# Two gate panels of the first mixer streamed through the head, with wider conditioning dots

## The chip, the core and the metric

The kernel runs on one core of a Trainium2 chip. The metric is the device time of one execution in microseconds (us). Three runs of the kernel before took 2177.68 to 2180.78 us, median 2178.91. Five engines work side by side, each through its own list in order: PE (matrix products), DVE (vector), ACT (ScalarE, functions and copies), POOL, and SP, which here only issues transfers.

## What is computed

A trunk of two layers over x of 256 rows and 2048 columns, with a condition c. Only the first half of layer 0 matters here:

```
shift, scale, gate, ... = split(silu(c) @ ada_w + ada_b)
h  = x * (1 + scale) + shift
xa, ga, ub, vb = split(h @ w_in)            # 1024 columns each
ya = rg_lru(conv(xa)) * gelu(ga)
yb = gelu(ub) * spatial(layer_norm(gelu(vb)))
x  = layer_norm(alpha * x + (1 + gate) * (concat(ya, yb) @ w_out))
```

Then an FFN, and a second layer with another mixer. All weights are fp32, and the largest ones are read once, so every weight passes from memory through the chip in the order in which it is used.

## The kernel before

A product is done in panels of 512 columns (`nb`) and chunks of 512 rows of the weight (`ch`); one weight block of a panel and a chunk is 1 MB. Such a block is loaded into one of the four buffers of `p_raw` (`load_raw`), and split into a high and a low part (`split`, L84 on ACT and L85 on DVE, two halves of 1024 columns each). PE then does three products a piece (`products`, L161 to L163), 24 for a block with its two halves of rows (`tb`). A few blocks aren't split but multiplied in fp32 (`products32`, L152).

The conditioning vectors (`mods`) are made by **dots**: `ada_dot` loads 1 MB of `ada_w` into a buffer of the same four, multiplies it by `silc` on DVE and sums each row; it does so in two halves of 1024 columns (L99), and `ada_final` adds the two sums and the bias (L104 to L109).

Mixer 0 (`mixer_ab`) begins with the **head**: 16 blocks of rows (`kb`), four to a chunk. For each block two dots give scale and shift, x is modulated on DVE (L545), and PE adds six fp32 products to six PSUM banks that stay open (panels 0, 1 and 6; L547: a head group). From the second chunk on, `stream` takes the panels 7, 4 and 5 for the chunk before, one behind each of the first three blocks: products into one of two banks `hs`, then a copy (first chunk, ACT, L524) or an add (DVE, L526) into an accumulator in SBUF, and a gelu after the last chunk. Behind the head the three streams run for the fourth chunk.

Then `linear` runs over the two **gate panels** 2 and 3, chunks in the order 2, 3, 0, 1, adding up in PSUM; its first two blocks are fp32 products (`RAW_GA`). Between the blocks `todo` places the convolution inputs, the two halves of the recurrence (`rg_lru`, on ACT and DVE), the norm (`v_norm`) and the spatial products. `evac` multiplies the gate into y. Then comes the **output projection** (`out_proj`): 16 blocks, the first two in fp32, the last four in `close`.

After each block `pump` asks for `RATE_E` = 1.0 more dots of the list `early` (24 dots: the gate of this half, and the first quarter of the next scale and shift); what is left is done two steps before the projection's end. The framework's scheduler sets the order on each engine from the order of the code and its own estimates; the engines then follow it strictly.

Of the kernel before, what the change touches and what calls it, by code (L numbers as in the profile page):

```python
# [13 lines left out]
P = 128  # L14
# [12 lines left out]
RATE_E = 1.0  # L27
QUIET = 2
RAW_GA = (0, 1)
# [13 lines left out]
def trunk_kernel(ctx, tc, I, out):  # L43
# [50 lines left out]
    def ada_dot(acc, l, idx, kb):  # L94
        w = p_raw.tile([P, D], F32, name="w")
        nc.sync.dma_start(w, I["ada_w"][l, idx, kb])
        for hf in range(2):
            cs = slice(hf * 1024, hf * 1024 + 1024)
            V.scalar_tensor_tensor(w[:, cs], w[:, cs], 1.0, silc[:, cs], op0=ALU.mult, op1=ALU.mult,  # L99
                                   accum_out=acc[:, hf:hf + 1])  # L100

    def ada_final(acc, l, s, nm, idx, k0, n):
        m = mods[l, s, nm][:, k0:k0 + n]
        V.tensor_tensor(m, acc[:, :, 0], acc[:, :, 1], op=ALU.add)  # L104
        bias = vc("ab", (6 * l + idx) * KB + k0, n)
        if nm == "sh":
            V.tensor_tensor(m, m, bias, op=ALU.add)
        else:
            V.scalar_tensor_tensor(m, m, 1.0, bias, op0=ALU.add, op1=ALU.add)  # L109
        ln = 2 * l + s - 1  # L110
        if nm == "sh" and ln >= 0:
            sc = mods[l, s, "sc"][:, k0:k0 + n]
            t4 = p_t.tile([P, n], F32, name="t4")
            V.tensor_tensor(t4, vc("nb", ln * 16 + k0, n), sc, op=ALU.mult)
            V.tensor_tensor(m, m, t4, op=ALU.add)
            V.tensor_tensor(sc, sc, vc("ng", ln * 16 + k0, n), op=ALU.mult)

    def ada_tiles(l, s, part, q, n=CH):
        for nm, idx in (("sc", 3 * s + 1), ("sh", 3 * s)) if part == "s" else (("gt", 3 * s + 2),):
            acc = p_t.tile([P, n, 2], F32, name="ga")  # L120
            for j in range(n):
                ada_dot(acc[:, j], l, idx, n * q + j)
                if j == n - 1:
                    ada_final(acc, l, s, nm, idx, n * q, n)
                yield
# [52 lines left out]
    def acc_bank():  # L178
        return psum["acc"].tile([P, NB], F32, name="acc")
# [316 lines left out]
    def mixer_ab(pump):  # L496
        with ExitStack() as st:
# [13 lines left out]
            dst = {7: vg[:, :, NB:], 4: ug[:, :, 0:NB], 5: ug[:, :, NB:]}  # L511

            with tc.tile_pool(name="pshead", bufs=1, space=PSUM) as p8, tc.tile_pool(name="hraw", bufs=3) as p_hr:
                head = [(nb, tb) for nb in (0, 1, 6) for tb in range(2)]
                banks = {k: p8.tile([P, NB], F32, name=f"hd{k[0]}{k[1]}") for k in head}

                def stream(nb, ch):
                    hl = load_w(src(nb, ch))
                    for tb in range(2):
                        bk = p8.tile([P, NB], F32, name=f"hs{tb}")  # L520
                        products(bk, xs[ch], hl, tb, range(2), True, True)
                        d = dst[nb][:, tb]
                        if ch == 0:
                            A.activation(d, bk, AF.Copy)  # L524
                        else:
                            V.tensor_tensor(d, d, bk, op=ALU.add)  # L526
                        if ch == 3:
                            A.activation(d, d, AF.Gelu_apprx_tanh)

                spread(silc, 4, lambda i: p8.tile([P, NB], F32, name=f"hs{i % 2}"), AF.Silu)  # L530
                for kb in range(KB):
# [31 lines left out]
                for nb in (7, 4, 5):  # L563
                    stream(nb, 3)
                    pump()
# [38 lines left out]
            def evac(nb, tb, bk):  # L604
                j = nb - 2
                ts = slice(tb * P, tb * P + P)
                e = p_t.tile([P, NB], F32, name="t512")
                A.activation(e, bk, AF.Gelu_apprx_tanh)
                pt = transposed(e, 4)
                V.tensor_tensor(y[j][:, :, ts], y[j][:, :, ts], pt, op=ALU.mult)  # L610
# [22 lines left out]
            def v_norm():  # L633
                for tb in range(2):
# [6 lines left out]
            todo = {1: lambda: (conv_in(0), conv_in(1)), 2: lambda: rg_lru(0), 4: v_norm,  # L641
                    5: lambda: (spatial(0), spatial(1)), 6: lambda: rg_lru(1)}
            count = [0]

            def pump2():
                count[0] += 1
                pump()
                if count[0] in todo:
                    todo[count[0]]()
# [140 lines left out]

    class Pump:
# [123 lines left out]
```

## Time and profile before

| | |
|---|---|
| three runs | 2177.68, 2178.91, 2180.78 us |
| profiled execution: span | 2175.9 us (its own time is not listed beside it; the runs' median lies 3.0 us above this span) |
| PE busy | 2111.6 us, 97% |
| DVE busy | 1618.6 us, 74% |
| ACT busy | 966.5 us, 44% |
| moved by DMA | 601.20 MB, mean 276 GB/s |

How the rows further below are read. On the page, a slice is a fortieth of the span, and a digit is a busy share in tenths. A row of the stages has the stretch and its length, the busy time of PE, PEld (weight loads), DVE, ACT and POOL with the number of instructions, the granted clock of PE as a share of full speed, the share of the DMA engines and GB/s. A row of a timeline or of the chain has start and length in us, then engine, line, operation and what is written from what, and in brackets the idle time before it with its releaser. A row of the groups has the count, busy us and mean ns, then the idle time before. A row of the waits has who waited for whom: us in total, how often, the longest.

### The profile page before, as it was taken

The page shows a single profiled execution, that of the slowest core. Times are in us where ns is not written, and L with a number is a line of the kernel's source. Part 1 is how long each engine was busy: PE and PEld are TensorE (multiplying, and loading weights), DVE is VectorE, ACT ScalarE, POOL GpSimd, SP SyncE. Part 2 cuts the span into 40 slices and gives each one's busy share as a digit, 9 for nine tenths or more (in the row PEclk, how much of TensorE's full clock was granted, in tenths as well). Part 3 has the DMA queues.
Part 4 walks back from the last instruction along what each step waited for, and adds up shares of the span by engine and source line. Part 5 has one row for each costly group of instructions (what it writes and reads, how often), then busy time and mean ns, then how long its engine had stood idle before and what let it go on. Part 6 is the DMA issues. An engine that isn't in the chain of part 4 may idle for free.

```text
span 2175.9 us, 24074 instructions
## 1 busy us (share of the span) xinstructions
PE 2111.6 (97%) x9124; PEld 1666.4 (77%) x9124; DVE 1618.6 (74%) x2202; ACT 966.5 (44%) x1124; POOL 31.5 (1%) x55
## 2 busy tenths in 40 slices
PE   7989999999999999999999999999999999999996
PEld 3556767887888888888868777868888888888885
DVE  7778988899977788889779977666555555555656
ACT  1215733544544445444444556354444444444442
POOL 0000000000000000000000011000000000000000
PEclk9999999999999999999999999999999999999998
DMA  9987787988888888888858877646676666555552
GB/s 399 388 322 267 303 329 297 341 325 336 301 314 312 322 330 322 335 319 312 319 217 311 324 267 292 261 173 221 230 271 229 222 226 233 208 203 193 194 194 91
DMA packets 84747, 601.20 MB, mean 276 GB/s; under 512 B 9444, under 2 KB 9876, under 8 KB 13846
## 3 DMA queue, kind: packets, MB, share of 16 engines
q1 hardware_dynamic: 84630, 599.67, 73.7%
q8 instruction: 71, 1.16, 0.2%
q14 instruction: 46, 0.37, 0.1%
HBM read 597.51 MB, written 2.12 MB: 276 GB/s over the span
## 4 chain that ended last, share of the span: by engine, by line
PE 85%; DVE 9%; ACT 2%; DMA 2%; issue 1%; POOL 1%; SPq 0%; DVEq 0%; ACTq 0%; POOLq 0%
PE acc L162 25%; PE acc L163 25%; PE acc L161 24%; DVE w L99 3%; PE hd L547 3%; PE acc L152 3%; DVE l L85 2%; PE aux L228 2%; DMA w<-in_ada_w 1%; PE hs L162 1%; PE hs L163 1%; PE hs L161 1%; DMA w<-in_w_cd 0%; ACT h L84 0%; POOL z L736 0%
## 5 line engine op out<-in xcount | busy, mean ns | idle before, releaser
L85 DVE TENSOR_TENSOR l<-w,h 128x1024 fp32r<-128x1024 f32 x676 | 822.9, 1223 | 421.4 <-ACT h L84 420.1
L84 ACT ACTIVATE h<-w 128x1024 fp32r<-128x1024 f32 x676 | 711.6, 1059 | 862.0 <-PE acc L163 689.4
L162 PE MATMUL acc<-l,xh 128*128 128x512 f32 x2608 | 1019.2, 391 | 6.2 <-DVE l L85 5.8
L161 PE MATMUL acc<-h,xh 128*128 128x512 f32 x2608 | 1018.2, 392 | 5.9 <-ACT xh L318 4.5
L163 PE MATMUL acc<-h,xl 128*128 128x512 f32 x2608 | 1018.3, 391 | 0.0
L162 PEld LDWEIGHTS acc<-l,xh 128*128 128x128 f32 x2608 | 489.8, 188 | 112.4 <-DVE l L85 11.8
L161 PEld LDWEIGHTS acc<-h,xh 128*128 128x128 f32 x2608 | 489.5, 188 | 108.2 <-ACT xh L318 5.5
L163 PEld LDWEIGHTS acc<-h,xl 128*128 128x128 f32 x2608 | 489.8, 188 | 100.4 <-DVE xl L319 0.3
L99 DVE SCALAR_TENSOR_TENSOR w<-w,silc 128x1024 f32<-128x1024 f32 x384 | 459.0, 1219 | 18.0 <-DMA w<-in_ada_w 15.6
L547 PE MATMUL hd<-w,y 128*128 128x512 f32 x192 | 93.8, 642 | 20.7 <-DVE y L545 20.7
L547 PEld LDWEIGHTS hd<-w,y 128*128 128x128 f32 x192 | 38.4, 205 | 72.7 <-issue 43.2
L85 DVE TENSOR_TENSOR xl<-hid,xh 128x1024 fp32r<-128x1024 f32 x44 | 53.9, 1224 | 34.2 <-ACT xh L84 33.6
L84 ACT ACTIVATE xh<-hid 128x1024 fp32r<-128x1024 f32 x44 | 46.8, 1063 | 63.0 <-PE acc L162 63.0
L152 PE MATMUL acc<-w,hx 128*128 128x512 f32 x96 | 43.1, 599 | 2.8 <-ACT hx L313 2.7
L161 PE MATMUL hs<-h,xh 128*128 128x512 f32 x96 | 40.9, 428 | 0.0
L162 PE MATMUL hs<-l,xh 128*128 128x512 f32 x96 | 39.0, 406 | 0.0
L163 PE MATMUL hs<-h,xl 128*128 128x512 f32 x96 | 38.0, 396 | 0.0
L84 ACT ACTIVATE xh<-y 128x1024 fp32r<-128x1024 f32 x12 | 12.7, 1058 | 56.6 <-DVE y L545 48.6
L152 PEld LDWEIGHTS acc<-w,hx 128*128 128x128 f32 x96 | 17.6, 190 | 23.4 <-issue 17.5
L99 DVE DVE_READ_ACCUMULATOR w<-w,silc 128x1 f32 x384 | 31.3, 82 | 0.0
L152 PE MATMUL acc<-w,y 128*128 128x512 f32 x64 | 28.5, 592 | 0.0
L427 DVE TENSOR_TENSOR hid<-hid,acc 128x512 f32<-128x512 f32 x40 | 27.2, 683 | 1.5 <-PE acc L163 1.4
(207 smaller groups left out, 851.4 us busy)
## 6 DMA issues: line engine op xcount, KB each, us to landing
w<-in_ada_w SPq DMA_DIRECT2D x192, 1024.0 KB, 5.1
w<-in_wg SPq DMA_DIRECT2D x88, 1024.0 KB, 5.2
w<-in_wu SPq DMA_DIRECT2D x88, 1024.0 KB, 5.1
w<-in_wd SPq DMA_DIRECT2D x88, 1024.0 KB, 4.9
w<-in_w_cd SPq DMA_DIRECT2D x32, 1024.0 KB, 6.2
w<-in_w_ab SPq DMA_DIRECT2D x20, 1024.0 KB, 5.2
w<-in_w_ab_out SPq DMA_DIRECT2D x16, 1024.0 KB, 7.0
w<-in_w_cd_out SPq DMA_DIRECT2D x16, 1024.0 KB, 6.7
```

The costliest lines, as they stand in the source:

```text
L84: A.activation(h, src, AF.Copy)
L85: mark["v"] = V.tensor_tensor(l, src, h, op=ALU.subtract)
L99: V.scalar_tensor_tensor(w[:, cs], w[:, cs], 1.0, silc[:, cs], op0=ALU.mult, op1=ALU.mult, accum_out=acc[:, hf:hf + 1])
L152: T.matmul(bk, x[:, k, ts], w[:, k], start=first and k == 0, stop=last and k == 3)
L161: T.matmul(bk, xh[:, k, ts], h[:, j], start=first and k == 0, stop=False)
L162: T.matmul(bk, xh[:, k, ts], l[:, j], start=False, stop=False)
L163: T.matmul(bk, xl[:, k, ts], h[:, j], start=False, stop=last and k == 3)
L228: T.transpose(pt[:, i], src[:, i * P:(i + 1) * P], ident)
L427: V.tensor_tensor(part(nb, tb), part(nb, tb), bk, op=ALU.add)
L547: T.matmul(banks[nb, tb], xt[:, k, tb * P:tb * P + P], w[:, i // 2], start=kb == 0, stop=kb == KB - 1)
```

## The change

- The gate panels 2 and 3 are streamed in the head too: each gets an SBUF accumulator (`ga`, in the buffer of the later row `gb`). Behind the four blocks of a chunk now stand panel 7, panel 4, panels 5 and 2, and panel 3. `RAW_GA` and the loop over the gate panels go; their blocks are all split.
- Behind the head the fourth chunk of the five panels runs with the banks of the later pool (`acc_bank`), with the recurrence, norm and spatial products between; `gate_y` multiplies both gates into y at the end.
- x is modulated on ACT (L541 of the new kernel) instead of DVE.
- A dot is one instruction of 2048 columns (L96), and `ada_final` has one operation less.
- `RATE_E` is 1.6, and the load of x is issued after three pumps of the output projection.

```
-RATE_E = 1.0
+RATE_E = 1.6
-        for hf in range(2):
-            cs = slice(hf * 1024, hf * 1024 + 1024)
-            V.scalar_tensor_tensor(w[:, cs], w[:, cs], 1.0, silc[:, cs], op0=ALU.mult, op1=ALU.mult,
-                                   accum_out=acc[:, hf:hf + 1])
+        V.scalar_tensor_tensor(w, w, 1.0, silc, op0=ALU.mult, op1=ALU.mult, accum_out=acc)
...
-        V.tensor_tensor(m, acc[:, :, 0], acc[:, :, 1], op=ALU.add)
...
-            dst = {7: vg[:, :, NB:], 4: ug[:, :, 0:NB], 5: ug[:, :, NB:]}
+            ga = p_row.tile([P, 2, 2, NB], F32, name="gb")
+            dst = {7: vg[:, :, NB:], 4: ug[:, :, 0:NB], 5: ug[:, :, NB:], 2: ga[:, 0], 3: ga[:, 1]}
...
-                    V.tensor_scalar(xt[:, k], xt[:, k], sc, sh, op0=ALU.mult, op1=ALU.add)
+                    A.activation(xt[:, k], xt[:, k], AF.Identity, scale=sc, bias=sh)
...
                     if k == 3:
                         xs.append(xs_split(xt))
-                    elif ch > 0:
-                        stream((7, 4, 5)[k], ch - 1)
+                    if ch > 0:
+                        for nb in ((7,), (4,), (5, 2), (3,))[k]:
+                            stream(nb, ch - 1, lambda tb: p8.tile([P, NB], F32, name=f"hs{tb}"))
...
-                for nb in (7, 4, 5):
-                    stream(nb, 3)
-                    pump()
...
+            def gate_y(j):
+                for tb in range(2):
+                    pt = transposed(ga[:, j, tb], 4)
+                    ys = y[j][:, :, tb * P:tb * P + P]
+                    V.tensor_tensor(ys, ys, pt, op=ALU.mult)
...
-            todo = {1: lambda: (conv_in(0), conv_in(1)), 2: lambda: rg_lru(0), 4: v_norm,
-                    5: lambda: (spatial(0), spatial(1)), 6: lambda: rg_lru(1)}
...
-            linear([(2, 3)], (2, 3, 0, 1), src, lambda gi, ch: xs[ch], evac, pump=pump2,
-                   raw=lambda gi, ci, nb: y[2 + ci] if ci < 2 and 2 * ci + nb - 2 in RAW_GA else None)
+            steps = {7: lambda: rg_lru(0), 5: v_norm, 2: lambda: (spatial(0), spatial(1))}
+            conv_in(0)
+            conv_in(1)
+            for nb in (7, 4, 5, 2, 3):
+                stream(nb, 3, lambda tb: acc_bank())
+                pump()
+                if nb in steps:
+                    steps[nb]()
+            rg_lru(1)
+            gate_y(0)
+            gate_y(1)
             x = p_res.tile([P, 2, D], F32, name="x")
-            nc.sync.dma_start(x, I["x"])
-            return x, out_proj(0, y, x, I["w_ab_out"], pump, (0,))
+            hook = Hook(pump, {3: lambda: nc.sync.dma_start(x, I["x"])})
+            return x, out_proj(0, y, x, I["w_ab_out"], hook, (0,))
```

What the change makes of the order of DVE is seen at three places. In these rows `w,ga<-w,silc` is a dot, `l<-w,h` the split of half a weight block, `m00sc` and `m00sh` the scale and shift.

**Block 9 of the head on DVE, before** (`hs_507` and `hs_521` are the two banks of the stream of panel 7 that stands ahead of its group on PE):

```order
L99 SCALAR_TENSOR_TENSOR w,ga<-w,silc 128x1024 x2
L526 TENSOR_TENSOR x<-x,hs_507 128x512
L104 TENSOR_TENSOR m00sh<-ga 128x1
L107 TENSOR_TENSOR m00sh<-m00sh,vec 128x1
L545 TENSOR_SCALAR y_112<-y_112,m00sc,m00sh 128x256
L85 TENSOR_TENSOR l<-w,h 128x1024
L526 TENSOR_TENSOR x<-x,hs_521 128x512
```

The same block with the change (the banks are now `hs_548` and `hs_562`):

```order
L518 TENSOR_TENSOR x<-x,hs_548 128x512
L96 SCALAR_TENSOR_TENSOR w,ga<-w,silc 128x2048
L518 TENSOR_TENSOR x<-x,hs_562 128x512
L102 TENSOR_TENSOR m00sh<-ga,vec 128x1
L84 TENSOR_TENSOR l<-w,h 128x1024 x2
```

The shift's sum stood between the two adds; now it stands behind both, and the modulation that needs it is gone from DVE's list.

**DVE between the splits, behind the head, before** (first half of the recurrence; `xc` is the convolution, `ii` a factor of the recurrence):

```order
L85 TENSOR_TENSOR l<-w,h 128x1024
L580 SCALAR_TENSOR_TENSOR xc<-xat_1083,vec,xc 128x256
L99 SCALAR_TENSOR_TENSOR w,ga<-w,silc 128x1024 x2
L85 TENSOR_TENSOR l<-w,h 128x1024
L597 TENSOR_TENSOR ii<-ii,xc 128x1024
L99 SCALAR_TENSOR_TENSOR w,ga<-w,silc 128x1024 x2
L85 TENSOR_TENSOR l<-w,h 128x1024
```

With the change, from the norm's sums to the first split of panel 2 (its last row; the split ahead of it, of panel 5, stands five rows above the first one):

```order
L628 BN_STATS vs_119<-x 128x6
L628 BN_STATS vs_120<-x 128x6
L284 BN_AGGR mv<-vs_119 128x2
L96 SCALAR_TENSOR_TENSOR w,ga<-w,silc 128x2048
L593 SCALAR_TENSOR_TENSOR rt<-ra,rt 128x1024
L286 TENSOR_SCALAR rs<-mv 128x1
L630 SCALAR_TENSOR_TENSOR x<-x,mv,rg 128x1024
L594 TENSOR_TENSOR ii<-ii,rt 128x1024
L631 SCALAR_TENSOR_TENSOR x<-x,rs,rb 128x1024
L596 SCALAR_TENSOR_TENSOR y_110<-ra,ii 128x256 x4
L284 BN_AGGR mv<-vs_120 128x2
L84 TENSOR_TENSOR l<-w,h 128x1024
```

The norm and the end of the first recurrence moved into one place, between the splits of two panels.

**DVE in the output projection, before** (splits of the projection's blocks and dots):

```order
L99 SCALAR_TENSOR_TENSOR w,ga<-w,silc 128x1024 x2
L85 TENSOR_TENSOR l<-w,h 128x1024 x2
L99 SCALAR_TENSOR_TENSOR w,ga<-w,silc 128x1024 x2
L104 TENSOR_TENSOR m00gt<-ga 128x4
L109 SCALAR_TENSOR_TENSOR m00gt<-m00gt,vec 128x4
L85 TENSOR_TENSOR l<-w,h 128x1024 x2
```

The same place with the change:

```order
L84 TENSOR_TENSOR l<-w,h 128x1024 x2
L96 SCALAR_TENSOR_TENSOR w,ga<-w,silc 128x2048 x2
L104 SCALAR_TENSOR_TENSOR m00gt<-ga,vec 128x4
L84 TENSOR_TENSOR l<-w,h 128x1024 x2
L96 SCALAR_TENSOR_TENSOR w,ga<-w,silc 128x2048
L84 TENSOR_TENSOR l<-w,h 128x1024 x2
```

One dot stood between the splits of two blocks; now it is one or two.

## Rows read from the trace of the kernel before

**Rows 1.** The page, busy time and slices.

```profile
PE 2111.6 (97%) x9124; PEld 1666.4 (77%) x9124; DVE 1618.6 (74%) x2202; ACT 966.5 (44%) x1124; POOL 31.5 (1%) x55
...
PE   7989999999999999999999999999999999999996
```

**Rows 2.** The stages: three chunks of the head, gate panels, projection, all the rest.

```profile
45.45:86.30 40.85, 37.30 (x120) 22.55 (x120) 31.07 (x60) 11.32 (x15) 0.00 (x0) 0.99 1.00 409
86.30:132.15 45.85, 40.74 (x121) 23.48 (x121) 34.49 (x66) 6.96 (x7) 0.00 (x0) 0.94 0.84 333
132.15:174.60 42.45, 41.38 (x125) 23.63 (x125) 30.54 (x54) 9.91 (x13) 0.00 (x0) 0.96 0.76 293
174.60:262.00 87.40, 82.71 (x353) 61.37 (x354) 79.62 (x135) 58.27 (x89) 4.79 (x5) 0.98 0.80 303
262.00:345.00 83.00, 78.05 (x328) 57.14 (x327) 72.61 (x109) 30.49 (x35) 0.00 (x0) 1.00 0.86 334
...
366.00:2176.00 1810.00, 1779.00 (x7935) 1449.15 (x7933) 1321.95 (x1680) 834.24 (x951) 24.69 (x41) 1.00 0.72 265
```

**Rows 3.** Timeline of PE in the head, head groups alone.

```profile
56.16 5.32 PE L547 MATMUL hd<-w,y 128*128 128x512 f32 x12
66.80 5.32 PE L547 MATMUL hd<-w,y 128*128 128x512 f32 x12
...
86.30 8.30 PE L547 MATMUL hd<-w,y 128*128 128x512 f32 x12 [3.54 <-DVE y L545]
...
132.15 7.11 PE L547 MATMUL hd<-w,y 128*128 128x512 f32 x12 [2.73 <-DVE y L545]
```

**Rows 4.** The chain of waits ahead of the groups of blocks 10 and 15.

```profile
110.76 0.69 DVE ug L526
111.55 0.42 DVE y L545
112.02 5.42 PE hd L547 x12
...
169.25 5.35 PE hd L547 x12
```

**Rows 5.** Groups of instructions, 0 to 380 us, ACT and DVE.

```profile
L84 ACT ACTIVATE h<-w 128x1024 fp32r<-128x1024 f32 x68 | 68.9, 1051 | 97.2 <-DMA w<-in_w_ab_out 40.9 <-DMA w<-in_w_ab 40.3 <-PE acc L163 11.1
L578 ACT ACTIVATE xc<-xat,vec 128x256 f32<-128x256 f32 x8 | 4.3, 589 | 0.1
...
L545 DVE TENSOR_SCALAR y<-y,m00sc,m00sh 128x256 f32<-128x256 f32 x16 | 6.6, 413 | 0.6
```

**Rows 6.** Timeline of DVE: two half dots, two kinds of split, the last dot's sum.

```profile
17.55 1.22 DVE L99 SCALAR_TENSOR_TENSOR w<-w,silc 128x1024 f32<-128x1024 f32 x1 [3.64 <-DMA w<-in_ada_w]
...
18.70 1.22 DVE L99 SCALAR_TENSOR_TENSOR w<-w,silc 128x1024 f32<-128x1024 f32 x1
...
170.00 1.23 DVE L85 TENSOR_TENSOR xl<-y,xh 128x1024 fp32r<-128x1024 f32 x1 [1.42 <-ACT xh L84]
...
300.30 2.36 DVE L85 TENSOR_TENSOR l<-w,h 128x1024 fp32r<-128x1024 f32 x2 [1.27 <-ACT h L84]
...
341.71 0.16 DVE L115 TENSOR_TENSOR m01sh<-m01sh,t 128x4 f32<-128x4 f32 x1
```

**Rows 7.** Timeline of PE: the first transposes behind the projection's products.

```profile
364.52 0.60 PE L228 MATMUL aux<-ident,x 128*128 128x128 f32 x4
```

**Rows 8.** Groups on DVE, 174.6 to 341.8 us.

```profile
L99 DVE SCALAR_TENSOR_TENSOR w<-w,silc 128x1024 f32<-128x1024 f32 x48 | 56.8, 1217 | 0.3 <-DMA w<-in_ada_w 0.3
...
L269 DVE SCALAR_TENSOR_TENSOR x<-x,t 128x512 f32<-128x512 f32 x4 | 2.6, 680 | 0.0
```

**Rows 9.** Waits: DVE from 174.6 to 345 us, PE from 174 to 380.

```profile
DVE l L85 <- ACT h L84: 11.1, 8, 2.4
DVE xc L580 <- ACT xc L578: 3.4, 1, 3.4
...
PE acc L162 <- DVE l L85: 4.9, 6, 1.9
```

More of the change, by code (lines that the diff above doesn't have):

```diff
@@ L26 @@
 WINDOWS = (2, 4, 8, 16)
-RATE_E = 1.0
+RATE_E = 1.6
 QUIET = 2
-RAW_GA = (0, 1)
 RAW_OUT = (0, 1)
@@ L96, in ada_dot @@
         nc.sync.dma_start(w, I["ada_w"][l, idx, kb])
-        for hf in range(2):
-            cs = slice(hf * 1024, hf * 1024 + 1024)
-            V.scalar_tensor_tensor(w[:, cs], w[:, cs], 1.0, silc[:, cs], op0=ALU.mult, op1=ALU.mult,
-                                   accum_out=acc[:, hf:hf + 1])
+        V.scalar_tensor_tensor(w, w, 1.0, silc, op0=ALU.mult, op1=ALU.mult, accum_out=acc)
     def ada_final(acc, l, s, nm, idx, k0, n):
         m = mods[l, s, nm][:, k0:k0 + n]
-        V.tensor_tensor(m, acc[:, :, 0], acc[:, :, 1], op=ALU.add)
         bias = vc("ab", (6 * l + idx) * KB + k0, n)
         if nm == "sh":
-            V.tensor_tensor(m, m, bias, op=ALU.add)
+            V.tensor_tensor(m, acc, bias, op=ALU.add)
         else:
-            V.scalar_tensor_tensor(m, m, 1.0, bias, op0=ALU.add, op1=ALU.add)
+            V.scalar_tensor_tensor(m, acc, 1.0, bias, op0=ALU.add, op1=ALU.add)
         ln = 2 * l + s - 1
@@ L119, in ada_tiles @@
         for nm, idx in (("sc", 3 * s + 1), ("sh", 3 * s)) if part == "s" else (("gt", 3 * s + 2),):
-            acc = p_t.tile([P, n, 2], F32, name="ga")
+            acc = p_t.tile([P, n], F32, name="ga")
             for j in range(n):
-                ada_dot(acc[:, j], l, idx, n * q + j)
+                ada_dot(acc[:, j:j + 1], l, idx, n * q + j)
                 if j == n - 1:
@@ L510, in mixer_ab, with stream @@
             xa_sb = [y[j].rearrange("p (t a) b -> p t (a b)", t=2) for j in range(2)]
-            dst = {7: vg[:, :, NB:], 4: ug[:, :, 0:NB], 5: ug[:, :, NB:]}
+            ga = p_row.tile([P, 2, 2, NB], F32, name="gb")
+            dst = {7: vg[:, :, NB:], 4: ug[:, :, 0:NB], 5: ug[:, :, NB:], 2: ga[:, 0], 3: ga[:, 1]}
+            def stream(nb, ch, bank):
+                hl = load_w(src(nb, ch))
+                for tb in range(2):
+                    bk = bank(tb)
+                    products(bk, xs[ch], hl, tb, range(2), True, True)
+                    d = dst[nb][:, tb]
+                    if ch == 0:
+                        A.activation(d, bk, AF.Copy)
+                    else:
+                        V.tensor_tensor(d, d, bk, op=ALU.add)
+                    if ch == 3:
+                        A.activation(d, d, AF.Gelu_apprx_tanh)
             with tc.tile_pool(name="pshead", bufs=1, space=PSUM) as p8, tc.tile_pool(name="hraw", bufs=3) as p_hr:
@@ L515, in mixer_ab @@
                 banks = {k: p8.tile([P, NB], F32, name=f"hd{k[0]}{k[1]}") for k in head}
[L517 to L528, printed above, removed]
                 spread(silc, 4, lambda i: p8.tile([P, NB], F32, name=f"hs{i % 2}"), AF.Silu)
@@ L602, in rg_lru @@
                     V.tensor_tensor_scan(y[j][:, i], ra[:, i], ii[:, i], 0.0, op0=ALU.mult, op1=ALU.add)
[L604 to L610, printed above, removed]
+            def gate_y(j):
+                for tb in range(2):
+                    pt = transposed(ga[:, j, tb], 4)
+                    ys = y[j][:, :, tb * P:tb * P + P]
+                    V.tensor_tensor(ys, ys, pt, op=ALU.mult)
             def spatial(j):
@@ L639, in v_norm @@
                     V.scalar_tensor_tensor(vg[:, tb], vg[:, tb], rs, rb, op0=ALU.mult, op1=ALU.add)
-            todo = {1: lambda: (conv_in(0), conv_in(1)), 2: lambda: rg_lru(0), 4: v_norm,
-                    5: lambda: (spatial(0), spatial(1)), 6: lambda: rg_lru(1)}
-            count = [0]
-            def pump2():
-                count[0] += 1
-                pump()
-                if count[0] in todo:
-                    todo[count[0]]()
-            linear([(2, 3)], (2, 3, 0, 1), src, lambda gi, ch: xs[ch], evac, pump=pump2,
-                   raw=lambda gi, ci, nb: y[2 + ci] if ci < 2 and 2 * ci + nb - 2 in RAW_GA else None)
+            steps = {7: lambda: rg_lru(0), 5: v_norm, 2: lambda: (spatial(0), spatial(1))}
[3 more added lines that the diff above has]
+                stream(nb, 3, lambda tb: acc_bank())
+                pump()
+                if nb in steps:
[3 more added lines that the diff above has]
+            gate_y(1)
             x = p_res.tile([P, 2, D], F32, name="x")
-            nc.sync.dma_start(x, I["x"])
-            return x, out_proj(0, y, x, I["w_ab_out"], pump, (0,))
+            hook = Hook(pump, {3: lambda: nc.sync.dma_start(x, I["x"])})
+            return x, out_proj(0, y, x, I["w_ab_out"], hook, (0,))
     def mixer_cd(ln, x, resid, pump):
@@ L789, in mixer_cd, with __init__, __call__ @@
             return out_proj(1, y, x, I["w_cd_out"], pump)
+    class Hook:
+        def __init__(self, pump, todo):
+            self.gen, self.pump, self.todo, self.count = pump.gen, pump, todo, 0
+        def __call__(self):
+            self.count += 1
+            self.pump()
+            if self.count in self.todo:
+                self.todo[self.count]()
     class Pump:
```

## The prediction

> **What bounds the kernel now.** The page comes first: PE is busy for 97% of the span and its slices read 9 nearly everywhere, except the first seven or so [rows 1]. So what can be gained lies early. The table of stages [rows 2] says how much: after 366 us PE is busy 1779.0 of 1810 us, and nothing of the change runs there but the wider dots, whose engine DVE has time over (1322 of 1810). Before 366 us there are three kinds of stretch. In the head (45.45 to 174.6) PE stands for some us in each of its three chunks, and DVE is busy for 31 to 34 of each 41 to 46 us. In the gate panels with the recurrence (174.6 to 262) and in the output projection (262 to 345) DVE is busy 79.6 of 87.4 and 72.6 of 83 us: there DVE is as full as PE.
>
> Where PE waits in the head is seen in its timeline [rows 3]: a head group and the stream behind it follow each other every 10.64 us, but at the start of chunks 2 and 3 PE waits 3.54 and 2.73 us for the modulated x, and the group after it takes 8.30 and 7.11 us instead of 5.32. That is the lower of its two clock levels, 1.2 GHz, which the wait has brought about. At smaller joints the chain [rows 4] shows what is in the way: DVE first adds the last bank (0.69 us), finishes the shift, modulates (0.42 us), and only then does PE go on.
>
> **Part 1, the head.** A head group takes 5.2 us and a stream 5.4 (together the 10.64). A chunk held four groups and three streams; from the second chunk on it now holds four and five: 4 x 10.64 + 5.4 = 48.0 us of PE. The long waits with their slow clock go, since panel 3 now stands at the chunk's end. What stays are joints at which the shift's sum stands behind an add on DVE (the order around block 9 shows it): add 0.69, sum 0.16, modulation on ScalarE. The trace has no such modulation; the nearest rows are the same form in the recurrence, 0.589 us, and DVE's own, 0.413 [rows 5]. I take the first, its exact form. With some 0.15 for the crossing that makes 1.6 us, or 1.15 where PE has two products of the next stream ahead (0.45). There are one of 1.6 and two of 1.15 in the second chunk, one of 1.15 in the third, and 1.4 where the first chunk's copies stand ahead of the modulation on ScalarE: 6.5 us together. Block 4's group should start 1 us sooner (modulation off DVE, fewer sums), at 44.3. Then 44.3 + 49.4 + 51.9 + (42.6 + 1.15) puts the end of block 15's group at 189.3 us, against 169.25 + 5.35 = 174.6 [rows 4]: 14.7 later, with five more blocks of panel work done. DVE (some 38 us of work in such a chunk of 52: the 34.5 of before [rows 2], two more panels at 3.5, less 12 small pieces and eight halves' overlap) and the DMA (13 loads of 1.05 MB, four of 0.79 and x, 17.3 MB, so 333 GB/s; the trace held 409 over the first chunk [rows 2]) are cover for all that is added there: the four splits and four adds of a chunk cost nothing, unless a load comes late.
>
> The ScalarE page of the Trainium skill (ScalarE: Activation LUTs, Rules for kernel authors) says that multiplications and additions belong on VectorE. The rows agree that ScalarE is slower, by 0.18 us a piece; where it stands on the path, at five joints, following that rule would give back 0.9 us of the sum, and DVE would carry 16 x 0.4 us more.
>
> **Part 2, from the head to the last dot.** After that PE has little and DVE much. PE's work from block 15's end is two panels less, while DVE's list is nearly the old one. Counted in the order from the split of the fourth x chunk to the last dot's sum, DVE has 30 splits where it had 42, 12 adds from PSUM where it had 6, 24 dots of 2048 where it had 48 of 1024; the 24 convolution steps, scans, gates and norms are the same. Prices are the starts of one behind the other: 1.14 us a split (two take 2.36, one 1.22), 1.15 a half dot (17.55 to 18.70) [rows 6], 0.60 an add (0.68 [rows 8] less the same overlap). A dot of 2048 isn't in the trace: between 2.15 (four times what 512 columns add, no fixed part) and 2.30 (two halves); I take 2.22, since from 512 to 1024 columns a piece grows by 1.217 - 0.680 = 0.537 [rows 8], so one of 2048 lasts 1.217 + 1.074 = 2.29, less the overlap of 0.07. So -13.7 + 3.6 - 1.9, and -0.5 for six sums: 12.5 us less. Before, this stretch ran from 171.2 (170.00 + 1.23) to 341.9 [rows 6], 170.6 us, of which DVE waited 18, 11.1 for splits whose load came late and 3.4 for the convolution's start [rows 9]. With the same waits it takes 158, with none 140.
>
> The VectorE page of the Trainium skill (VectorE: DVE Perf Modes, The TRN2 errata) says that the fixed latency is paid once for one large tile and once for each of many small ones; its fp32 figure puts that at 157 ns. The rows show 1.22 us of length but 1.15 from start to start, so they give half of that; by the page's figure this sum would be about 2 us shorter.
>
> The split that opens this stretch ended 2.0 us after block 15's group began (169.25 to 171.23); that group now begins at 184.1, and with an add and a split ahead of it I take 187.1. I take 5 of the 18 us of waiting away: the convolution's and those on PE's last products go, since PE is now ahead, but in the projection each split still waits for its load (1.27 in [rows 6]), at 2.6 loads a block instead of 2. So the last dot's sum is at 187.1 + 153 = 340.1, against 341.9.
>
> **Part 3, after the last dot.** In the order all dots now stand ahead of the last 12 splits, which were 8: six blocks are left on PE instead of four. The rate of 1.6 does that: the projection has 16 dots to take in where it had 13, and takes them in its first ten blocks. Before, PE ended 22.7 us after the last sum (364.52 [rows 7]); two blocks of 5.4 more make 33.5. PE ends the projection at 373.6, against 364.5: 9 us later. From there on PE has no wait that the wider dots could shorten, and I cost the rest at nothing; if that cover were gone, 136 later dots could give 0.08 us each.
>
> The two first gate blocks were fp32 products (16 pieces, 6.9 us by a head group's 12 in 5.2) and are now split (5.4): that frees 3 us of PE, where PE waits for DVE, so it counts nothing. x is now asked for behind three pumps; its first reader is the first evacuation, some 30 us later, so nothing either. The table loads on ScalarE rise by a few of 1.28 us and stand beside DVE's work.
>
> **The sum.** +9 us on the profiled execution's span of 2175.9. Its own time isn't listed; the median of the three runs, 2178.9, lies 3.0 above that span, and I add to it: 2188. A measurement here can tell about 0.2%, 4.4 us, from no change.
>
> **Rivals.**
> First, the loads decide. In the projection a block now has 2.6 loads, 2.73 MB. At the 334 GB/s of that stage [rows 2] this is 8.2 us, against some 7.2 that I give DVE for it (2.3 split, 3.5 dots, 1.4 wait). Over seven blocks and with all 18 us of waiting kept, 5 + 7 = 12 us more: 2193 to 2200. For it: ScalarE waited 40.9 us for the projection's loads [rows 5]. Against: 409 GB/s were reached in the head.
> Second, DVE follows without a wait. Then the last sum is at 327, PE ends at 361, and the time is 2175 to 2179: no difference. For it: PE runs ahead of DVE, so none of its products are waited for. It needs loads that are always early, which no stage had.
> Third, faster: PE sets the end again. Its place is the head: if the 6.5 us of joints vanish too (the sums slip in front of the adds) and DVE has no wait behind it, the stretch begins at 180.6, the last sum is at 320.6, PE ends at 354.2 and the time is 2168.5. It decides when the last dot's sum is done before 327 (364.5 - 33.5 - 4.4). For it: PE's own work from block 15's end is only some 136 us (14 split blocks 76, two fp32 blocks 14, six streams 33, the rest 13). Against: the adds stand ahead of the sums in the order, and DVE's 140 us are a floor.
>
> **How the numbers follow.** Forecast 0.45, loads 0.20, no waits 0.20, faster 0.15. So slower by over 0.2%: 0.65; within 0.2%: 0.20; faster: 0.15. The range 2173 to 2201 holds the first three cases, and leaves out most of the faster one and the ends of the loads'; a dot at 2.30 instead of 2.22 adds 2 us, at 2.15 takes 2, both inside. The forecast's own range is 2183 to 2194.
>
> **What would show it.** Right: block 15's group ends between 186 and 193; chunks of 50 to 53 us without a slow group; behind panel 5's last chunk PE waits some 10 us for the split of panel 2, because two dots, the norm and the scans stand ahead of it on DVE (15 us in the order, with 4 of PE's work beside them), where the longest PE wait for a split was 1.9 us [rows 9]; DVE over 90% busy from 187 on; the last dot's sum near 340 and then six blocks without a DVE wait. Wrong: a last sum before 327, or a PE that stays busy from 190 to 300. The dot's row should read 2.2 to 2.3 us, ScalarE's modulation 0.59.

## The result and the profile after

The changed kernel takes 2201.93 us (median of four runs, 2201.0 to 2203.43), the kernel before 2179.85 beside it (2177.68 to 2183.89): a ratio of 1.0096, 95% interval 1.0081 to 1.0111. Slower was forecast, but by 9 us, and it is 22. The median lies 0.9 us above the upper end of the range; by the ratio, on the 2178.9 from which the prediction started, it is 2199.8.

The two profiled executions differ by 25.8 us (span 2201.7 against 2175.9). In each run of the changed kernel the time lies 1.7 above the span, so the span before belongs to that kernel's fastest run (2177.68, 2.2 below the median); the one profiled after was its slowest (2203.43, 1.5 above). 3.7 us of the 25.8 are the luck of two runs. By milestones:

| | before | forecast | after | later by |
|---|---|---|---|---|
| block 15's group ends | 174.6 | 189.3 | 192.7 | 18.1 |
| last early dot's sum | 341.9 | 340.1 | 344.6 | 2.7 |
| projection's products end | 364.5 | 373.6 | 378.1 | 13.6 |
| first products of the FFN | 380.65 | +9 | 398.31 | 17.7 |
| span | 2175.9 | +9 | 2201.7 | 25.8 |

The projection's end is the start of what PE does next or, where PE waits there, its last product's end less the 0.2 us by which neighbours overlap.

The page of the changed kernel, as [rows 1], and below it the two groups that answer to [rows 5] and [rows 8]:

```profile
PE 2115.5 (96%) x9140; PEld 1675.5 (76%) x9140; DVE 1596.7 (73%) x1746; ACT 983.3 (45%) x1150; POOL 35.2 (2%) x55
...
PE   7999779999999999999999999999999999999997
...
L96 DVE SCALAR_TENSOR_TENSOR w<-w,silc 128x2048 f32<-128x2048 f32 x192 | 438.4, 2286 | 44.9 <-DMA w<-in_ada_w 40.0
...
L541 ACT ACTIVATE y<-y,m00sh,m00sc 128x256 f32<-128x256 f32 x16 | 9.6, 598 | 77.7 <-DVE m00sh L102 77.7
```

PE's busy time has hardly changed; two slices behind the head, which read 9 before, read 7. Its stages (columns as in [rows 2]):

```profile
45.00:192.70 147.70, 142.42 (x481) 90.79 (x482) 101.72 (x117) 47.10 (x59) 0.00 (x0) 0.99 0.90 355
192.70:262.00 69.30, 57.34 (x243) 41.92 (x243) 62.26 (x95) 46.30 (x70) 3.66 (x5) 0.90 0.62 230
262.00:345.00 83.00, 68.61 (x278) 50.18 (x277) 76.76 (x88) 33.61 (x45) 0.00 (x0) 0.94 0.85 331
```

In the head PE now stands for 5 of 148 us. Behind it, it stands for 12 of 69 and 14 of 83, with DVE at 90% in the first and 92% in the second: that is where the panel work taken out of this stretch went.

The joints of the head, in PE's timeline, as [rows 3], and the chain of waits ahead of the second, as [rows 4]:

```profile
95.97 5.42 PE L543 MATMUL hd<-w,y 128*128 128x512 f32 x12 [1.17 <-ACT y L541]
108.44 5.42 PE L543 MATMUL hd<-w,y 128*128 128x512 f32 x12 [1.57 <-ACT y L541]
```

```profile
104.19 0.69 DVE x L518
104.87 2.21 DVE w L96 x2
107.08 0.07 DVE x L518
107.15 0.45 issue
107.60 0.17 DVE m00sh L102
107.77 0.02 issue
107.79 0.61 ACT y L541
108.40 0.04 issue
108.44 1.13 PE hd L543 x2
```

PE's wait is 1.57 us, near the 1.6 forecast, but the chain is another one: between the first add and the shift's sum stands the whole dot, 2.21 us. Whether the dot is late for its place in the list or for its load, the chain doesn't tell; the part on fewer bytes below comes back to it.

The table of waits, PE from 190 to 345 us, as [rows 9], and its stages of 10 us around the longest wait:

```profile
PE acc L156 <- ACT h L83: 13.9, 3, 8.0
PE acc L157 <- DVE l L84: 8.5, 6, 3.3
```

```profile
220.00:230.00 10.00, 6.49 (x28) 4.67 (x26) 10.00 (x15) 9.90 (x16) 0.00 (x0) 0.99 0.93 348
230.00:240.00 10.00, 4.22 (x13) 2.79 (x13) 9.87 (x15) 9.66 (x13) 1.46 (x1) 0.50 0.34 127
240.00:250.00 10.00, 8.02 (x38) 6.21 (x39) 10.00 (x13) 1.83 (x3) 1.53 (x1) 1.00 0.79 268
```

The wait of 8.0 us stands between panel 5 and panel 2, where one of about 10 us was forecast. DVE is full there (10.00, 9.87, 10.00), but PE waits first for ScalarE, which from 212 us on changes its table seven times; four of these loads, and a gelu between two of them, from its timeline:

```profile
218.49 1.28 ACT L520 ACT_TABLE_LOAD   x1
219.78 0.63 ACT L520 ACTIVATE ug<-ug 128x512 f32<-128x512 f32 x1
220.42 1.28 ACT L584 ACT_TABLE_LOAD   x1
...
227.19 1.28 ACT L520 ACT_TABLE_LOAD   x1
...
229.14 1.28 ACT L592 ACT_TABLE_LOAD   x1
```

The gelus of the panels (L520) and the recurrence (L584 to L592) take turns, and the copies of the split stand behind both. After the wait PE works at a granted clock of 0.50, the lower of its two levels.

Two rows of DVE bound its list, as [rows 6]: from the end of the split of the fourth x chunk (190.5) to the last dot's sum (344.6) it takes 154.1 us, forecast 153. DVE is busy for 138.7 of them and idle for 15.4, forecast 140 and 13:

```profile
189.31 1.22 DVE L84 TENSOR_TENSOR xl<-y,xh 128x1024 fp32r<-128x1024 f32 x1
...
344.43 0.16 DVE L110 TENSOR_TENSOR m01sh<-m01sh,t 128x4 f32<-128x4 f32 x1
```

Last, DVE in the closing stage. Ahead of the norm's aggregate, on which the transposes wait, stands a whole dot, and the aggregate starts when it is done:

```profile
374.91 2.27 DVE L96 SCALAR_TENSOR_TENSOR w<-w,silc 128x2048 f32<-128x2048 f32 x1
377.11 0.08 DVE L96 DVE_READ_ACCUMULATOR w<-w,silc 128x1 f32 x1
377.11 0.26 DVE L284 BATCH_NORM_AGGREGATE mv<-st 128x2 f32<-128x24 f32 x1
```

and PE's two waits for it, the first as [rows 7]:

```profile
379.88 0.63 PE L223 MATMUL aux<-ident,x 128*128 128x128 f32 x4 [1.63 <-issue]
...
390.56 1.07 PE L223 MATMUL aux<-ident,x 128*128 128x128 f32 x8 [2.37 <-DVE x L299]
```

### The profile page after: what moved, and what is told of

It reads as the page before. It is cut to its first block, busy times and chain, and to the rows that moved or that the text cites. A ratio compares the mean times of both kernels' runs of the same rounds, so it can differ in the third digit from the quotient of the medians.

```text
span 2201.7 us, 23617 instructions
## 1 busy us (share of the span) xinstructions
PE 2115.5 (96%) x9140; PEld 1675.5 (76%) x9140; DVE 1596.7 (73%) x1746; ACT 983.3 (45%) x1150; POOL 35.2 (2%) x55
## 4 chain that ended last, share of the span: by engine, by line
PE 84%; DVE 7%; ACT 3%; DMA 3%; issue 2%; POOL 1%; DVEq 0%; SPq 0%; POOLq 0%; ACTq 0%
PE acc L157 24%; PE acc L158 24%; PE acc L156 24%; PE hd L543 4%; DMA w<-in_ada_w 2%; DVE w L96 2%; PE aux L223 2%; DVE l L84 2%; PE acc L147 2%; PE hs L158 1%; PE hs L157 1%; PE hs L156 1%; PE hs L166 0%; DMA rg<-in_w_pool 0%; POOL z L727 0%
## 5 line engine op out<-in xcount | busy, mean ns | idle before, releaser
L96 DVE SCALAR_TENSOR_TENSOR w<-w,silc 128x2048 f32<-128x2048 f32 x192 | 438.4, 2286 | 44.9 <-DMA w<-in_ada_w 40.0
L156 PE MATMUL hs<-h,xh 128*128 128x512 f32 x120 | 50.7, 422 | 1.9 <-DVE ug L518 1.3
L157 PE MATMUL hs<-l,xh 128*128 128x512 f32 x120 | 48.1, 401 | 0.0
L158 PE MATMUL hs<-h,xl 128*128 128x512 f32 x120 | 46.9, 391 | 0.0
L541 ACT ACTIVATE y<-y,m00sh,m00sc 128x256 f32<-128x256 f32 x16 | 9.6, 598 | 77.7 <-DVE m00sh L102 77.7
L156 PEld LDWEIGHTS hs<-h,xh 128*128 128x128 f32 x120 | 22.5, 188 | 9.7 <-DVE ug L518 2.1
L314 DVE TENSOR_TENSOR xl<-t,xh 128x512 fp32r<-128x512 f32 x18 | 12.4, 688 | 22.1 <-ACT xh L313 22.1
```

The lines of the kernel that those rows point to most:

```text
L96: V.scalar_tensor_tensor(w, w, 1.0, silc, op0=ALU.mult, op1=ALU.mult, accum_out=acc)
L156: T.matmul(bk, xh[:, k, ts], h[:, j], start=first and k == 0, stop=False)
L157: T.matmul(bk, xh[:, k, ts], l[:, j], start=False, stop=False)
L158: T.matmul(bk, xl[:, k, ts], h[:, j], start=False, stop=last and k == 3)
L314: r["end"] = V.tensor_tensor(l_[:, :, ts], hx, h[:, :, ts], op=ALU.subtract)
L541: A.activation(xt[:, k], xt[:, k], AF.Identity, scale=sc, bias=sh)
```

## The experiments

Twelve kernels were run, each beside the kernel before on the same chip; its medians there lay between 2181.4 and 2181.8. "a" is built on the changed kernel, "b" on the kernel before. Stage by stage, from the profiles (close: what is lost against the kernel before between the projection's end and the FFN; later: from there to the end):

| run | median us | ratio, interval | head ends | projection ends | close | later |
|---|---|---|---|---|---|---|
| before | 2179.9 | | 174.6 | 364.5 | | |
| after | 2201.9 | 1.0096 (1.0081 to 1.0111) | 192.7 | 378.1 | 4.1 | 8.2 |
| a_halves | 2209.0 | 1.0142 (1.0120 to 1.0163) | 194.3 | 388.4 | 0.5 | 5.3 |
| b_wide | 2183.5 | 1.0016 (1.0006 to 1.0026) | 175.1 | 364.5 | 0.0 | 5.6 |
| a_dve | 2205.7 | 1.0112 (1.0095 to 1.0130) | 193.6 | 381.7 | 4.1 | 8.3 |
| a_head | 2209.0 | 1.0126 (1.0108 to 1.0143) | 210.2 | 387.5 | 4.1 | 6.9 |
| a_mixed | 2197.7 | 1.0069 (1.0054 to 1.0083) | 191.8 | 377.0 | 0.7 | 8.0 |
| a_short | 2188.0 | 1.0028 (1.0018 to 1.0038) | 192.8 | 367.6 | 0.0 | 6.5 |
| a_shared | 2180.0 | 0.9991 (0.9982 to 1.0000) | 177.2 | 354.9 | 5.4 | 7.8 |
| a_raw | 2200.8 | 1.0087 (1.0073 to 1.0101) | 192.2 | 376.9 | 5.3 | 3.9 |
| a_buf5 | 2210.5 | 1.0132 (1.0114 to 1.0150) | 196.3 | 384.4 | 5.3 | 10.4 |
| b_buf5 | 2183.3 | 1.0012 (1.0003 to 1.0021) | 176.6 | 368.8 | 0.0 | 1.0 |
| b_act | 2181.8 | 0.9999 (0.9989 to 1.0009) | 172.0 | 365.3 | 0.0 | 6.5 |
| b_shared | 2162.2 | 0.9912 (0.9895 to 0.9928) | 151.3 | 338.7 | 0.0 | 3.4 |

The last column comes from one execution each and says little below some 6 us. From 166 us on, b_act has the same instructions in the same order as the kernel before, and nearly the same median as its runs beside it; it still loses 6.5 us there, because its profiled execution was the longest of its twelve runs, and that of the kernel before the shortest of its four.

The first theory was that the undivided dot, in the head's chain and in the close, took what the forecast had not counted; its rival, that the loads did.

**The parts of the change alone: a_halves, b_wide, a_dve, b_act.**

```
a_halves (back to two halves)   b_wide: the opposite edit on the kernel before
-        V.scalar_tensor_tensor(w, w, 1.0, silc, ..., accum_out=acc)
+        for hf in range(2):
+            V.scalar_tensor_tensor(w[:, cs], w[:, cs], 1.0, silc[:, cs], ..., accum_out=acc[:, hf:hf + 1])
a_dve                            b_act: the opposite edit on the kernel before
-                    A.activation(xt[:, k], xt[:, k], AF.Identity, scale=sc, bias=sh)
+                    V.tensor_scalar(xt[:, k], xt[:, k], sc, sh, op0=ALU.mult, op1=ALU.add)
```

a_halves: 

> The changed kernel with the dots in two halves of 1024 columns again, all else as changed. Theory: of the 22 us that the change costs, some 13 arise before the projection's products end, since DVE's list is longer there than PE's, and the rest later, because a dot of 2.2 us that can't be parted stands in the closing stages and in the attention ahead of short pieces that PE waits for. Then the first part stays (about 2 us more DVE work) and most of the later 12 us go: 2188 to 2194 us. Rival: the later loss comes from another order of the scheduler that has nothing to do with the width; then 2199 to 2205.

b_wide: 

> The kernel before with dots of 2048 columns and nothing else of the change. Theory (an undivided dot delays the short pieces behind it): slower by 6 to 12 us, 2186 to 2192. Rival (15 us of DVE work less in all, order does not matter): 2176 to 2180.

a_dve: 

> The changed kernel with x modulated on DVE again. Theory: the head's joints are set by the add and the sum on DVE, ScalarE adds 0.2 us at five of them, DVE has time for 6.6 us more there: 2200 to 2203, no difference. Rival: the crossing to ScalarE is what the joints cost (PE waited 14.5 us for it in 8 waits): 4 to 8 us faster, 2194 to 2198.

b_act: 

> The kernel before with the modulation of x on ScalarE instead of DVE. Theory (in the changed kernel it gained 3.8 us against DVE because DVE's list in the head is relieved): the head ends 1 to 4 us earlier, the whole 2176 to 2180. Rival (the modulation was hidden, and the gain there lay in the order): 2179 to 2184, as the kernel before.

In halves the changed kernel is 7 us slower, not faster: the theory fell. The halves lose 10 us by the projection's end and win 3.6 back in the close (0.5 against 4.1). Of the 10, 1.6 are the head's and 3.2 longer work on DVE; the rest is idle time in DVE's list, whose cause stays open. So the wide dot is worth having early, and costs in the close. In the kernel before the wide dots move nothing ahead of the FFN and cost 2 to 3.5 us in all. With the modulation back on DVE the changed kernel is 3.8 us slower by the medians, but the intervals overlap; in the kernel before it makes no difference on either engine, though the head then ends 2.6 us sooner: what the head gained was lost again before the projection's end. What is left is the streaming of the panels, together with the rate of 1.6, the new places of the recurrence and the norm, and the later load of x; no run takes one of these alone.

**Dots moved into the head: a_head.** Of the 24 early dots, one is drawn behind each of blocks 1 to 3 of three chunks; these are nine, where the expectation says twelve, and eight more than in the changed kernel fall ahead of the head's end (40 dots in place of 32).

```
-RATE_E = 1.6
+RATE_E = 1.0
...
                         for nb in ((7,), (4,), (5, 2), (3,))[k]:
                             stream(nb, ch - 1, ...)
+                        if k:
+                            drain(pump.gen, 1)
```

> The changed kernel with 12 of the 24 early dots issued in the head, one behind each stream of the second to fourth block of a chunk, and the rate at 1.0. Theory: behind the head DVE sets the pace, so 12 dots (26.6 us of DVE) less there bring the end of the projection forward by 12 to 20 us, less what the head grows (0 to 5): 2182 to 2194 us. Rival: the loads set the pace; the bytes up to the projection's end are the same, and the head then needs 21.5 MB a chunk, 413 GB/s in 52 us: it grows by what is won behind it, 2198 to 2204.

The stretch from the head's end to the projection's end fell from 185.4 to 177.3 us, so DVE's list does count there; but the head grew by 17.5, and the whole is slower than either theory had it. DVE had time over in the changed kernel's head (101.72 of 147.70 above). The growth is as long as eight dots in DVE's list (8 x 2.21 = 17.7), so it doesn't single out the loads; the next runs went after them.

**Fewer bytes in the head: a_shared, b_shared.** Both leave out the shift's own weights: the shift dot multiplies the block that the scale dot left.

```
-        w = p_raw.tile([P, D], F32, name="w")
-        nc.sync.dma_start(w, I["ada_w"][l, idx, kb])
+        if l == 0 and idx == 0:
+            w = kept[0]
+        else:
+            w = kept[0] = p_raw.tile([P, D], F32, name="w")
+            nc.sync.dma_start(w, I["ada_w"][l, idx, kb])
```

a_shared: 

> The changed kernel with each shift dot of the head reading the block that its scale dot left in the buffer: 16 loads of 1 MB fewer, the same operations on every engine. The shifts are sums of other numbers. Theory (the loads through four buffers set the pace of the head): block 15's group ends at 175 to 184 in place of 192.7, the whole 2184 to 2194. Rival (the order in DVE's list, add, dot, shift's sum, and then the modulation, together with PE's work sets it): block 15's group ends at 188 to 193, the whole 2197 to 2203.

b_shared: 

> The kernel before with each shift dot of the head reading the block that its scale dot left in the buffer: 16 loads of 1 MB fewer, the same operations on every engine. The shifts are sums of other numbers. Theory (the bytes pace the head in the kernel before too, 62.3 MB in 174.6 us at 357 GB/s, so that each block added there costs its own 2.9 us): with 16.8 MB fewer the head falls to what PE has to do, 151.3 us busy in it, and block 15's group ends at 150 to 158; the whole falls by 10 to 20 us, to 2160 to 2172. Rival (the joints of DVE and PE hold the head of the kernel before, and the loads only follow): block 15's group ends at 168 to 175, the whole 2174 to 2182.

Both heads fell to what PE has to do. The stages, of a_shared and then of b_shared:

```profile
50.00:177.00 127.00, 127.00 (x444) 83.25 (x442) 99.19 (x114) 45.12 (x54) 0.52 (x1) 1.00 0.78 300
```

```profile
45.00:153.00 108.00, 108.00 (x350) 65.52 (x348) 96.59 (x187) 30.83 (x37) 0.67 (x3) 1.00 0.84 331
```

PE is busy for 127.00 of 127 and 108.00 of 108 us. Every operation is still there, the adds, the dots and the sums, and PE waits for none of them. Both heads end where their theories had them; a_shared's whole is lower than either had it.

That doesn't show that late loads made the joints, for with fewer loads the scheduler laid out the lists anew. In a_shared the shift's dot of the same block stands ahead of the first add; in the changed kernel it stands behind it (104.87 above). DVE's timeline in a_shared:

```profile
91.84 2.29 DVE L101 SCALAR_TENSOR_TENSOR w<-w,silc 128x2048 f32<-128x2048 f32 x1
...
94.63 0.69 DVE L523 TENSOR_TENSOR x<-x,hs 128x512 f32<-128x512 f32 x1 [0.50 <-PE hs L163]
95.24 0.15 DVE L107 TENSOR_TENSOR m00sh<-ga,vec 128x1 f32<-128x1 f32 x1
```

And in the changed kernel itself no dot waits for its load once 70 us have passed. DVE's waits there for the dots' loads from 14 to 70 us, and all its waits from 70 to 192 us:

```profile
DVE w L96 <- DMA w<-in_ada_w: 7.4, 6, 2.8
```

```profile
DVE l L84 <- ACT h L83: 13.6, 6, 5.7
DVE ug L518 <- PE hs L158: 11.2, 6, 2.5
DVE x L518 <- PE hs L158: 5.5, 3, 2.5
DVE xl L84 <- ACT xh L83: 4.5, 1, 4.5
DVE gb L518 <- PE hs L158: 4.0, 3, 2.6
```

From 23 to 70 us a dot starts within 0.2 us of its load's landing; after that, the landings that the trace gives (14 of 18) lie 3.6 to 10.8 us ahead of the dot. The kernel before is alike: 7.5 us of such waits up to 70 us, none from there to 174. So the loads pace the first 70 us. From there on DVE waits for PE's streams and ScalarE's copies, and what holds the joints is the order of the lists; that is read from the traces, and no run keeps the order and takes the loads away. In the first chunk a_shared gains 6.3 of its 15.5 us (block 4's group starts at 38.5 in place of 44.9), b_shared 4.3 of its 23.3. The whole heads, before and after, and the DMA from 10 to 80 us of the kernel before:

```profile
0.00:174.60 174.60, 151.34 (x421) 81.98 (x421) 128.53 (x262) 35.41 (x43) 0.62 (x8) 0.96 0.89 357
```

```profile
0.00:192.70 192.70, 173.60 (x537) 103.21 (x538) 130.14 (x166) 56.50 (x72) 0.62 (x8) 0.99 0.92 363
```

```profile
10.00:80.00 70.00, 59.27 (x162) 31.60 (x163) 52.81 (x110) 11.75 (x15) 0.00 (x0) 0.98 1.01 420
```

62.3 and 70.0 MB (length by rate) pass in the two heads, at nearly one mean rate. But the mean joins a full stretch (1.01, 420 GB/s) and the two chunks behind it, where the share is 0.84 and 0.76 [rows 2].

What the two runs do show is PE's own work. Without joints the change makes the head 25.9 us longer (151.3 to 177.2), which is the work of the five more blocks that stand ahead of that group (5 x 5.4 = 27). It grew by 18.1, so only 7.8 of the 23.3 us that the head of the kernel before lost were filled. And between these two runs the change still costs 17.9 us (2162.2 and 2180.0): what holds up the head is not the main reason that the changed kernel is slower.

**Bytes or buffers: a_buf5, b_buf5.** The head's shift dots get a buffer of their own, a fifth one.

```
-        w = p_raw.tile([P, D], F32, name="w")
+        own = l == 0 and idx == 0
+        w = (fifth[0] if own else p_raw).tile([P, D], F32, name="ws" if own else "w")
...
+                    tc.tile_pool(name="hdot", bufs=1) as fifth[0]:
```

a_buf5: 

> The changed kernel with a fifth weight buffer in the head, which the shift dots alone use. Theory (the bytes pace the head, 335 GB/s over a chunk): block 15's group ends at 189 to 193, the whole 2198 to 2203. Rival (the round trip through four buffers paces it, since the issuing queue waits for DVE to free one and the same bytes need only 45 us a chunk at the 386 GB/s seen elsewhere): block 15's group ends at 179 to 186, the whole 2186 to 2196.

b_buf5: 

> The kernel before with the same fifth buffer in the head. Theory (bytes pace the head): block 15's group ends at 172 to 175 (174.6 in the kernel before), the whole 2177 to 2182. Rival (the round trip through four buffers): block 15's group ends at 162 to 169, DVE's list behind it starts that much earlier, the whole 2168 to 2176, which would beat both kernels.

From block 4 to the head's end a_buf5 needs 146.1 us (50.2 to 196.3) against 147.8 (44.9 to 192.7), b_buf5 129.0 against 129.1. That doesn't settle bytes against buffers: the issuing queue works in order, and between 45 us and the head's end it stood before the loads into the fifth buffer, for 95.5 us in a_buf5 and 97.8 in b_buf5. The round trip was still there, through one buffer. In a_buf5, block 4 itself comes 5.3 us later, and the whole is slower than either theory had it; why the first chunk loads more slowly (352 GB/s over the first 45 us against 388) stays open. b_buf5 lies just above its first theory, by 1.6 us in the head and 1.3 in the whole.

**The list behind the head: a_short, a_raw.** a_short takes the 24 early dots over 128 columns only, with all their loads (15/16 of these sums are left out). a_raw leaves two blocks unsplit, as the kernel before did.

```
a_short
-        V.scalar_tensor_tensor(w, w, 1.0, silc, ..., accum_out=acc)
+        m = 128 if l == 0 and (idx == 2 or (idx in (3, 4) and kb < 4)) else D
+        V.scalar_tensor_tensor(w[:, :m], w[:, :m], 1.0, silc[:, :m], ..., accum_out=acc)
a_raw
+                raw = ch == 3 and nb in (4, 5)
...
+                    if raw:
+                        products32(bk, y[3], hl, tb, range(2), True, True)
```

a_short: 

> The changed kernel with the 24 early dots taken over 128 columns instead of 2048; their loads of 1 MB each are kept. It leaves out 15/16 of these sums. Theory (DVE's list behind the head sets the projection's end): some 2.1 us less for each of 24 dots, 50 us, far more than PE's idle time there (27 us between 192.7 and 378.2), so the last early dot's sum falls to 325 or before, the projection's end to 350 to 358, and the whole to 2174 to 2182. Rival (the loads of these dots, which hold the four buffers, set it): 2192 to 2200.

a_raw: 

> The changed kernel with the fourth chunk of the panels 4 and 5 multiplied in fp32, unsplit, as the kernel before did with two gate blocks: four splits of 1.15 us less on DVE and four on ACT behind the head, and PE longer by 1.7 us a block. Theory (DVE's list sets the projection's end): 2195 to 2200. Rival (PE's own work and ScalarE's set it): 2201 to 2206.

With 50 us taken from DVE's list the projection ends 10.5 us sooner (367.6), so DVE did hold it, but not alone. DVE's waits in a_short, and below them one of ScalarE's, 190 to 355 us:

```profile
DVE l L84 <- ACT h L83: 26.9, 11, 6.8
...
DVE w L97 <- DMA w<-in_ada_w: 8.6, 4, 3.5
```

```profile
ACT h L83 <- DMA w<-in_w_ab_out: 22.9, 5, 8.5
```

In the changed kernel DVE's first was 7.7 us, its second 0.7. ScalarE's copies, for which DVE waits, wait themselves for the projection's loads. So the copies and the loads stand right behind DVE, how much each holds is not separated, and the result fell between the two theories. a_raw is 1.1 us faster than the changed kernel, inside the intervals, and at the border of its two theories: it decides nothing.

**The dots behind the first mixer: a_mixed.** Wide in the head and among the early dots, in halves later.

```
+            wide = l == 0 and (s == 0 or (part == "s" and q == 0))
+            acc = p_t.tile([P, n, 1 if wide else 2], F32, name="gw" if wide else "ga")
```

> The changed kernel with the undivided dot kept in the head and in the 24 early dots; every later dot is in two halves again. Theory (the time lost behind the projection's end, 12 us of the 25.8, comes with the undivided dots that stand in DVE's list in the closing stage and in the attention of layer 1): projection's end as in the changed kernel (378), the closing stage loses under 1 us in place of 4.1, the whole 2192 to 2197. Rival (that loss comes with the moved start and whatever order the scheduler then finds, as the kernel with all dots in halves lost 5 there too): 2199 to 2206.

The close is as the theory had it: 0.7 us lost in place of 4.1, and the whole is 4.2 us faster than the changed kernel (the intervals just overlap), the best of its versions that leave nothing out. In DVE's timeline half a dot now stands where a whole one did:

```profile
373.85 1.21 DVE L99 SCALAR_TENSOR_TENSOR w<-w,silc 128x1024 f32<-128x1024 f32 x1
374.98 0.08 DVE L99 DVE_READ_ACCUMULATOR w<-w,silc 128x1 f32 x1
374.98 0.26 DVE L294 BATCH_NORM_AGGREGATE mv<-st 128x2 f32<-128x24 f32 x1
```

The later part is not: 8.0 us are lost there in a_mixed too. Its compiled lists are, over the last 60% of every engine's, the same as those of the kernel before. 4.3 of the 8.0 come from one place: a dot's load was late, and PE waited 2.6 us for the FFN's `sg`, which stood behind it on DVE. DVE's timeline, PE's waits and the stage of 5 us around them:

```profile
743.07 1.23 DVE L99 SCALAR_TENSOR_TENSOR w<-w,silc 128x1024 f32<-128x1024 f32 x1 [2.00 <-DMA w<-in_ada_w]
```

```profile
PE aux L233 <- DVE sg L411: 2.6, 1, 2.6
```

```profile
745.00:750.00 5.00, 2.76 (x9) 2.37 (x10) 5.00 (x7) 1.10 (x2) 0.00 (x0) 0.72 0.68 236
```

That differs from run to run (a_mixed: 2191.0 to 2201.8), and the profiled run of the kernel before had none of it.

Of the versions that leave nothing out none is faster than the kernel before.

## Why the prediction was right in its direction and short in its size

**Bound and mechanism: right.** DVE's list sets the projection's end, the gate panels' work leaves a stretch where PE had time over, and six blocks are left after the last dot instead of four. The last term came out as priced: PE ends 33.5 us after the last sum, forecast 33.5. The list was 154.1 us, forecast 153.

**Part 1, block 15's group: 3.4 us short.** It ended at 192.7, forecast 189.3: 0.6 in the first chunk, 1.7 and 1.1 in the next two (51.1 and 53.0 us where 49.4 and 51.9 stood), the third as forecast. PE's own work was priced right: where nothing waits, the three chunks take 48.0, 48.0 and 42.7 us (a_shared), forecast 48.0, 48.0 and 42.6. In the changed kernel the joints add 9.2 us to that, forecast 6.5. Most of the difference is the step that failed, "the long waits with their slow clock go": ahead of block 4, where no panel stands, PE still waits 2.71 us, and the group takes 7.11 us (5.42 in the kernel before, behind a wait as long). The other joints cost 1.3 to 1.8 each, where 1.15 to 1.6 stood; the 0.15 for the crossing came from no row, and the chain shows 0.06. "The DMA ... are cover for all that is added there" fails in the first 70 us, where the dots start as their loads land, and holds behind them. The rival of the loads, 2193 to 2200, is nearer to the result than the forecast, but it placed them in the projection, where DVE held the end and the loads stood behind it (a_short).

**Part 2, the last dot's sum: 4.5 us short,** 3.4 of it handed on from the head and 1.1 in the list. The dot itself came out as priced: 2.286 us long, 2.21 from start to start, against 2.29 and 2.22. Two halves at 1.15 become 2.21, so a pair saves 0.09. The Trainium skill (VectorE: DVE Perf Modes, The TRN2 errata) says that a fixed latency is paid once for each instruction; 157 ns is an estimate worked out from its fp32 formula. The rows give a little over half of that. ScalarE's modulation took 598 ns, forecast 589; moving it back to DVE costs 3.8 us by the medians (a_dve; the intervals overlap) and doesn't give 0.9 back. The Trainium skill (ScalarE: Activation LUTs, Rules for kernel authors) would have it on VectorE.

**Part 3, "I cost the rest at nothing": 12.3 us short in the profile.** This is the step that failed by most. 4.1 are the close: a dot twice as long stands ahead of the norm's aggregate. a_mixed shows it: 0.7 with halves. The forecast weighed the wide dots by their total on DVE alone, not by what queues behind one. Of the 8.2 that follow, 3.7 are the two profiled runs' distance from their medians. The largest step among the 8.2, 4.8 us, stands in the attention (24.5 later at 1365 us of the kernel before, 19.7 at 1296). Over the same stretch the seven other kernels with wide dots there lose 3.5 to 4.2 and the five with halves -0.2 to 2.9 (a_mixed 2.0, b_act 2.6). So some 2 us may go with the width, which is argued from this list alone, and the rest is inside what single executions differ by. By the medians a_mixed is 4.2 us faster, no more than its gain up to the FFN (4.4 in the profile). What makes the remainder stays open.

**What would show it.** Right were the group's end within 186 to 193, chunks of 50 to 53 us but for the slow group (block 4's took 7.11 us, against 5.42 in the kernel before), the long wait behind panel 5, DVE near 90% from there on, and the six blocks. Wrong was who makes PE wait behind panel 5: ScalarE's table changes, which were to "stand beside DVE's work". Since DVE was full through that wait, it moved no end. The rivals without DVE waits needed a last sum at 327 or before; it was at 344.6.

## What to carry to other kernels

An engine's idle time is filled only as far as what makes it idle allows: 7.8 of 23 us were, and the rest of the work that was moved into the head made it longer. Behind the head DVE's list, 16.5 us shorter but begun 19.3 us later, kept the last sum where it was (2.7 us later). An experiment that takes loads away can also change the order that a scheduler gives the lists: compare the lists, and compare each load's landing with the start of its reader, before naming either as the cause. And a longer instruction is priced by what queues behind it at the narrow places, not by its engine's total.

## What the runs showed of the hardware

A wait is paid for twice on PE: after the pause of 8 us the granted clock was 0.50 over 230 to 240 us, and over the whole stretch 192.7 to 262 it was 0.90 where [rows 2] had 0.98. In a_mixed a wait of 2.6 us lowered the clock to 0.72 over five microseconds, and the two together cost 4.3 us.

From 10 to 80 us of the kernel before the DMA was full, with a share of 1.01 at 420 GB/s; in the two chunks behind that it ran at 333 and 293 GB/s with shares of 0.84 and 0.76 [rows 2]. The 357 to 363 GB/s over a whole head are a mean of both, not the most that it gives.
